# Third x group of a hybrid attention layer: its square sums, roots, normalisations and turns placed anew, and two of the cosine and sine spreads issued later

## The chip, the cores and the metric

The kernel runs on one core of a Trainium2 chip. The core's engines work side by side, each through its own instructions in order: TensorE (PE in the profile; its weight loads are PEld), VectorE (DVE), ScalarE (ACT), GpSimd (POOL) and SyncE (SP, which here only issues DMAs). They wait for each other by semaphores. The metric is the device time of one execution in microseconds (us); lower is better. Three runs of the kernel before took 1143.2 to 1147.12 us, with a median of 1145.37.

## The reference

One decoder layer over x of 2048 rows by 1024 columns, float32:

```python
mod = jax.nn.silu(c) @ w_ada[l] + b_ada[l]
shift, scale, gate = jnp.split(mod, 3, axis=-1)
h = rms_norm(x, g_pre[l]) * (1.0 + scale[:, None, :]) + shift[:, None, :]
proj = h @ w_in[l]
qa, ka, va, fa, za, qb, kb, vb, zb = jnp.split(proj, split_points, axis=-1)
oa = forgetting_attention(qa, ka, va, fa + b_fgate[l]) * silu(za)      # 8 heads of 64
qb, kb = rope(qb, positions), rope(kb, positions)
ob = sliding_window_sink_attention(qb, kb, vb, sinks[l]) * silu(zb)    # 8 query heads, 2 key heads
y = jnp.concatenate([oa, ob], axis=-1) @ w_out[l]
x = x + gate[:, None, :] * rms_norm(y, g_post[l])
```

(Reshapes are left out of these lines.) For the change, the first three matter: each row of x is divided by its root mean square, then scaled and shifted by column, and `h` is multiplied with the columns of `w_in`, of which `kb`, `vb` (with the forget gates `fa`) and `zb0` come first.

## The kernel before

**Groups and tiles.** x is handled in 16 tiles of 128 rows, x0 to x15, and these in four groups of 512 rows: group 0 is x0 to x3, group 1 x4 to x7, group 2 (the third) x8 to x11, group 3 x12 to x15. For a group the kernel does, in this order:

- `load_x` (L414): one 512 KB DMA for each tile, on SP's queue.
- `squares` (L422): the sum of squares of each row of a tile, by one ScalarE instruction with an accumulator (L429) and the reading of it; given an engine, by one VectorE instruction (L431). Both write the squares themselves into one scratch tile, `junk`, of which there is a single buffer.
- `root` (L433): on GpSimd two small instructions, mean and epsilon (L436) and the power -0.5 (L437), for the tiles of a slice of the group.
- `normal` (L439): a tile is multiplied by its root on VectorE (L445).
- `turn_x` (L470), eight times: 128 columns of all four tiles are transposed by TensorE (four matmuls with the identity, L453, into a PSUM tile `px` of five). One tick later ScalarE scales and shifts them (L461), once for odd turns, twice for even ones, and another tick later VectorE makes the low half of the float16 pair `hT` (L466, for odd turns also the high half, L465). Projections read `hT` of the group: the k-th step of a projection needs the k-th turn.

**Slices.** The early part of the kernel is a list of small TensorE pieces, `punits`; each is a slice, and `fill` (L1180) issues them in order. Ahead of a slice go the events that were set for it: `at_slice(n, f)` and the steps of the weights. After every second slice (the odd ones) a tick runs what was deferred by `after(n, f)` (L202). So the order of work on each engine's queue is written out by hand by slice numbers: an engine meets its instructions in this order, and one that waits holds up those behind it.

**The list** (L1077 to L1103), for group ci = 0, 1, 2: eight units of `kb` (L361, three matmuls each; for ci = 0 seven of them are empty), eight units of `vb` (L854, 12 matmuls each), eight units of `zb0` (L361), for ci = 2 two more such sets, of `zb0` and `zb1`; and in between the eight turns of group ci + 1, behind the units numbered in `at_`. This makes slices 0 to 31, 32 to 63 and 64 to 111. Group 1 is turned in slices 16 to 31. In slices 32 to 63 come `kb` on group 1 (32 to 39), `vb` on group 1 from slice 40, and the turns of group 2 at slices 41, 44, 47, 50, 53, 56, 59 and 62; `kb` on group 2 begins at slice 64. Group 3 is turned from slice 81 on, and `kb` on group 3 begins at slice 112.

**Events in question**, by slice: squares of x8, x9, x10, x11 at 11, 14, 33, 34, all on ScalarE; root of group 2, for all four, at 35; its normalisations at 37, 38, 39, 40; squares of x12 to x15 at 48, 50, 52, 54 on ScalarE; root of group 3 at 57; its normalisations at 66, 68, 70, 72.

**Cosines and sines.** `spread` (L475) copies a group's 32 rows of cosine and sine to all 128 partitions: eight DMAs of 64 KB from SP's queue, at slices 12, 22 and 30 for groups 1, 2 and 3. The rotation of `kb` (`evac_rope`, L797) uses them: after the last unit ScalarE copies the sums out (`qf`, L807), SP swaps halves by four DMAs (`qs`, L809), VectorE multiplies by the cosine (L812), which frees the PSUM bank, and some ticks later by the sine (L822), adds (L823), and ends in `kst` by four more DMAs (L837). For group ci the cosine is wanted a few slices behind the last `kb` unit, at slices 39, 71 and 119. The three banks `bk` of PSUM go round: a unit set takes one, and the instruction that empties it frees it.

**The maximum of a weight block.** `add` (L1021) sets the steps of each weight block by slice. For `zb1` they are written out (L1040): load at 6, `w_max` at 38 (VectorE, L236, 1.21 us, then a small DMA out on GpSimd's queue, L239), `w_back` at 46 (a DMA back to all partitions, L244, which waits for the first), `w_scale` at 67 (VectorE, L255 and four small ones), and the splitting in float16 pairs at 71 to 77. `zb1` is used first after slice 96.

Of the kernel before, what the change touches and what calls it, by code (L numbers as in the profile page):

```python
# [43 lines left out]
def hybrid_layer(  # L44
# [17 lines left out]
    V, A, G, PE, SP = nc.vector, nc.scalar, nc.gpsimd, nc.tensor, nc.sync  # L62
# [20 lines left out]
    def sm(n, tag):  # L83
        return small.tile([P, n], F32, tag=tag, name=tag)
# [131 lines left out]
    def w_load(key, pieces, eng=None):  # L216
        raw = wpool.tile([P, KT, P], F32, tag="wraw", name=f"wr_{key}")
        o = 0
        for col0, n in pieces:
            (eng or G).dma_start(raw[:, :, o:o + n], w_in0[:, col0:col0 + n].rearrange("(k p) n -> p k n", p=P))  # L220
            o += n
        wq[key] = [raw]
# [11 lines left out]
    def w_max(key):  # L234
        mx = sm(1, "w_mx")
        V.tensor_reduce(mx[:], wq[key][0][:], axis=AX.XY, op=ALU.max, apply_absolute_value=True)  # L236
        md = mx_d[len(kaps_seen) % 3]
        kaps_seen.append(key)
        G.dma_start(md[:], mx[:])  # L239
        wq[key].append(md)  # L240

    def w_back(key):
        mxr = mxp.tile([P, P], F32, tag="mxr", name="mxr")
        G.dma_start(mxr[:], wq[key].pop().rearrange("p o -> (p o)").partition_broadcast(P))  # L244
        wq[key].append(mxr)

    def w_scale(key):

        floor = key[:2] == "qk"
        raw, mxr = wq[key]  # L250
        if key in first:
            mx2 = mxr
        else:
            mx2 = sm(1, "w_mx2")
            V.tensor_reduce(mx2[:], mxr[:], axis=AX.X, op=ALU.max)  # L255
        pw = sm(1, "w_pw")
        pow2_floor(pw[:], mx2[:], "w_p2")
        if floor:
            V.tensor_tensor(pw[:], pw[:], pfl[:], op=ALU.max)
        sw = sm(1, "w_sw")  # L260
        V.reciprocal(sw[:], pw[:])
        V.tensor_scalar(sw[:], sw[:], 2.0 ** 14, None, op0=ALU.mult)
        wq[key] = [raw, pw, sw]

    def w_high(key):
        raw, pw, sw = wq[key]
        width = VB if key == "vb" else P
        pool = vbw if key == "vb" else wpq if key[0] in "qk" else wpool
        if key[:2] == "va":
            j = int(key[2:])  # L270
            if j % 2 == 0:
                wv[j // 2] = fx["wv"].tile([P, 2, KT, 2 * P], F16, tag="whl", name=f"wh_va{j}")
            whl = wv[j // 2][:, :, :, (j % 2) * P:(j % 2 + 1) * P]
        elif key == "fa":
            whl = wq["vb"][:, :, :, P:]
        else:
            whl = pool.tile([P, 2, KT, width], F16, tag="whl", name=f"wh_{key}")
        A.activation(whl[:, 0, :, 0:raw.shape[-1]], raw[:], AF.Identity, scale=sw[:])
        wq[key].append(whl)
# [65 lines left out]
    def pieces(key):  # L345
        kind, j = key[:2], int(key[2:] or 0)
        if kind == "qk":
            return [(OFF_QA + j * 64, 64), (OFF_KA + j * 64, 64)]
        return [({"qb": OFF_QB, "va": OFF_VA, "za": OFF_ZA, "zb": OFF_ZB}[kind] + j * P, P)]
# [72 lines left out]
    def squares(ci, us=range(4), eng=None):  # L422
        if ci not in rstd:
            rstd[ci] = sm(4, "ss"), sm(4, "rst")
        for u in us:
            junk = hst.tile([P, D], BF16, tag="junk", name="junk", bufs=1)
            x_, sum_ = xt[ci * 4 + u], rstd[ci][0][:, u:u + 1]
            if eng is None:
                A.activation(junk[:], x_, AF.Square, accum_out=sum_)  # L429
            else:  # L430
                eng.scalar_tensor_tensor(junk[:], x_, 1.0, x_, op0=ALU.mult, op1=ALU.mult, accum_out=sum_)  # L431

    def root(ci, us=slice(0, 4)):  # L433
        ss, rst = (t[:, us] for t in rstd[ci])
        rv = sm(4, "rs_v")[:, us]
        G.tensor_scalar(rv, ss, 1.0 / D, EPS, op0=ALU.mult, op1=ALU.add)  # L436
        G.tensor_tensor(rst, rv, mhalf[:].broadcast_to([P, us.stop - us.start]), op=ALU.pow)  # L437

    def normal(ci, us=range(4), eng=None):  # L439
        for u in us:  # L440
            t, r = ci * 4 + u, rstd[ci][1][:, u:u + 1]
            if eng is A:
                A.activation(xt[t], xt[t], AF.Copy, scale=r)
            else:
                V.tensor_scalar(xt[t], xt[t], r, None, op0=ALU.mult)  # L445
# [24 lines left out]
    def turn_x(ci, k):  # L470
        scaled, split, _ = turn(ci, k)
        after(1, scaled)
        after(2, split)

    def spread(g):  # L475

        gr, gc = slice(32 * g, 32 * g + 32), slice(g * CH, (g + 1) * CH)
        for r in range(4):
            rr = slice(32 * r, 32 * r + 32)
            SP.dma_start(cosT[rr, gc], cs_[gr, :])  # L480
            SP.dma_start(sinT[rr, gc], (sp_ if r % 2 else sn_)[gr, :])
# [537 lines left out]
    pkeys, punits = [], []  # L1019

    def add(key, us):  # L1021
        if key in ("va01", "va23"):
            for j in key[2:]:
                add(f"va{j}", [])
        elif key not in pkeys and key not in ("kb", "vb"):
            at = len(punits) - {"za3": 4}.get(key, 20 if key[:2] == "za" else 0)
            for n, (lead, f) in enumerate(((42, lambda: w_load(key, pieces(key))), (31, lambda: w_max(key)),
                                           (21, lambda: w_back(key)), (12, lambda: w_scale(key)),
                                           (9, lambda: w_high(key)), (7, lambda: w_low(key, 0)),
                                           (5, lambda: w_low(key, 1)), (4, lambda: w_done(key)))):  # L1030
                if n >= 4 and key[:2] in ("qk", "za"):
                    lead -= 1
                if n < 4 and key == "qb0":
                    lead += (16, 14, 12, 4)[n]
                if key[:2] in ("zb", "va"):
                    lead += {"va0": 26, "va2": 26, "zb3": 18}.get(key, 8)
                if n == 0 and key in ("qk1", "za0"):
                    lead += 8
                if key == "zb1":
                    lead = at - (6, 38, 46, 67, 71, 73, 75, 77)[n]  # L1040
                if key == "zb0":
                    if n >= 3:
                        events.setdefault((11, 11, 13, 14, 15)[n - 3], []).append(f)
                else:
                    events.setdefault(max(at - lead, n), []).append(f)
        if key not in pkeys:
            pkeys.append(key)
        punits.extend(us)
# [10 lines left out]
    def at_slice(n, f):  # L1059
        events.setdefault(n, []).append(f)  # L1060
# [16 lines left out]
    for ci in range(NCH):  # L1077
        n0 = len(punits)
        if ci:
            add("kb", kb_units(ci))  # L1080
        else:
            add("kb", [lambda: None] * (KT - 1) + [ku[KT - 1]])
        add("vb", vb_units(ci))
        if ci < 3:
            add(*others[ci])
            if ci == 2:
                add(*others[4])
                add(*others[5])

            mine, punits[n0:] = punits[n0:], []  # L1090
            at_ = ([15, 17, 18, 19, 20, 21, 22, 23], [8, 10, 12, 14, 16, 18, 20, 22], [16, 18, 20, 22, 24, 26, 28, 30])[ci]
            for n, u in enumerate(mine):
                punits.append(u)
                if n in at_:
                    punits.append(lambda ci=ci, k=at_.index(n): turn_x(ci + 1, k))
            if ci < 2:

                for u in range(4):
                    if ci or u:
                        at_slice(n0 + 16 + 2 * u if ci else (11, 14, 33, 34)[u], lambda ci=ci, u=u: squares(ci + 2, (u,)))  # L1100
                    at_slice(len(punits) + 2 + 2 * u if ci else len(punits) + 5 + u, lambda ci=ci, u=u: normal(ci + 2, (u,)))
                at_slice(len(punits) - 7 if ci else len(punits) + 3, lambda ci=ci: root(ci + 2))
            at_slice((12, 22, 30)[ci], lambda ci=ci: spread(ci + 1))  # L1103
    n0 = len(punits)
    at_slice(n0, lambda: open_fox())
    at_slice(n0 + 8, gates)
# [590 lines left out]
    with tc.manual_schedule():  # L1697
# [35 lines left out]
        for s, stp_ in enumerate(steps):  # L1733
            hd, r = divmod(s, NS)
            w_acc += stp_.w
            lead = 14 + min(9, max(0, s - 100) * 3 // 8)
# [114 lines left out]
```

## Time and profile before

| what | value |
|---|---|
| median of 3 runs | 1145.37 us (1143.2 to 1147.12) |
| the profiled execution | 1145.31 us |
| its span on the core | 1143.6 us, with 25130 instructions |
| mean granted TensorE clock | 0.994 |
| TensorE busy | 1116.7 us (98%) |
| VectorE busy | 902.5 us (79%) |
| ScalarE busy | 661.4 us (58%) |
| GpSimd busy | 220.6 us (19%) |
| slices 32 to 63 on TensorE | 62.78 to 88.89 us from the span's start |

How to read it: times are microseconds from the start of the span. The span is the profiled core's time from the first to the last instruction; the execution's own time is 1.7 us longer. Ends of matmuls are modelled, since they are pipelined, so their starts are compared here. `L361` is a line of the kernel. `out<-in` names the tile written and those read. The granted clock is TensorE's, as a share of full speed. The chain that ended last is followed back from the last instruction, at each step to what released it or to the instruction before it on its engine.

### The profile page before, as it was taken

What the parts mean: (1) busy time and instruction counts of PE and PEld (TensorE: products, weight loads), DVE (VectorE), ACT (ScalarE), POOL (GpSimd) and SP (SyncE); (2) the same over time, 40 slices, a digit from 0 to 9 for tenths busy, and PEclk for the clock granted to TensorE, in tenths of its full rate; (3) what the DMA queues carried; (4) which work ended last, traced back from release to release, by engine and by line L of the source; (5) the groups of instructions that cost most, each with busy time, mean ns of one, the idle gap of its engine ahead of it and who ended that gap; (6) DMA issues with size and microseconds to landing.
All of it is one profiled execution on the core that took longest, in us unless ns stands there. A gap on an engine that the chain in (4) does not pass through costs nothing.

```text
span 1143.6 us, 25130 instructions
## 1 busy us (share of the span) xinstructions
PE 1116.7 (98%) x9854; PEld 656.6 (57%) x9854; DVE 902.5 (79%) x1982; ACT 661.4 (58%) x1151; POOL 220.6 (19%) x339
## 2 busy tenths in 40 slices
PE   7889999999999999999999999999999999999997
PEld 3666545667755856555555555555556565544444
DVE  8967468968878558889888899888888998666663
ACT  3966245655555412676767666666666888633332
POOL 3111135555556420010010111001000000100000
PEclk9989999999999999999999999999999999999999
DMA  9854254423232232443244332123311237687743
GB/s 364 269 154 86 75 102 88 93 60 94 69 76 84 58 93 51 82 103 46 63 64 89 84 67 71 38 49 52 69 41 48 77 98 213 146 235 196 203 132 111
DMA packets 124365, 119.83 MB, mean 105 GB/s; under 512 B 65977, under 2 KB 101858, under 8 KB 124246
## 3 DMA queue, kind: packets, MB, share of 16 engines
q1 hardware_dynamic: 113374, 85.73, 27.5%
q0 software_dynamic: 10720, 32.46, 13.6%
q8 instruction: 77, 1.26, 0.5%
q14 instruction: 42, 0.34, 0.1%
q10 hardware_dynamic: 152, 0.04, 0.0%
HBM read 64.49 MB, written 25.18 MB: 78 GB/s over the span
## 4 chain that ended last, share of the span: by engine, by line
PE 77%; DVE 13%; DMA 4%; ACT 3%; issue 2%; SPq 1%; POOL 0%; DVEq 0%; POOLq 0%; ACTq 0%
PE bk L361 30%; PE bk L1637 13%; PE bk L379 7%; PE sta L1410 4%; PE sta L1409 4%; PE bk L1360 4%; PE poa L1435 3%; PE poa L1436 2%; PE poa L1433 2%; DVE a_m L1363 2%; PE pss L948 2%; PE bk L854 2%; PE pob L1005 1%; DVE pha L1423 1%; DMA wr_kv<-in_w_in_dram 1%
## 5 line engine op out<-in xcount | busy, mean ns | idle before, releaser
L1416 ACT ACTIVATE p<-sta,lift,scl_qk 128x1024 f32<-128x1024 f32 (+2 forms) x160 | 171.8, 1074 | 126.1 <-PE sta L1410 78.7
L361 PE MATMUL bk<-hT,wh_qk 128*128 128x512 f16 x768 | 195.4, 379 | 0.0
L1423 DVE TENSOR_TENSOR pha<-p,pha 128x1024 f16<-128x1024 f32 (+2 forms) x160 | 168.9, 1056 | 0.6 <-ACT pha L1420 0.6
L1363 DVE TENSOR_REDUCE a_m<-bk 128x1 f32<-128x512 f32 x192 | 130.3, 685 | 45.8 <-PE bk L1360 44.9
L1637 PE MATMUL bk<-wohl,oz 128*128 128x512 f16 x744 | 163.6, 379 | 1.0 <-DVE oz L1587 0.7
L1420 ACT ACTIVATE pha<-p 128x1024 f16<-128x1024 f32 (+2 forms) x160 | 148.0, 925 | 6.4 <-PE poa L1436 1.8
L1637 PEld LDWEIGHTS <-oz 128*128 128x128 f16 x744 | 70.5, 98 | 84.7 <-DVE oz L1587 1.8
L1433 PE MATMUL poa<-vt,pha 128*128 128x65 f16 x1088 | 116.6, 193 | 1.6 <-DVE ona L1442 1.6
L1436 PE MATMUL poa<-vt,pha 128*128 128x65 f16 x1088 | 116.1, 193 | 0.6 <-DVE pha L1423 0.6
L1435 PE MATMUL poa<-vt,pha 128*128 128x64 f16 x1088 | 116.6, 195 | 0.0
L361 PEld LDWEIGHTS <-wh_qk 128*128 128x128 f16 x768 | 71.7, 97 | 73.8 <-issue 2.1
L1360 PE MATMUL bk<-T 66*128 66x512 f16 (+2 forms) x320 | 110.5, 349 | 1.9 <-DVE a_m L1363 1.7
L1409 PE MATMUL sta<-T 128*128 128x512 f16 (+1 forms) x320 | 111.0, 347 | 1.1 <-ACT p L1416 0.9
L1433 PEld LDWEIGHTS <-pha 128*128 128x128 f16 x1088 | 101.5, 96 | 16.1 <-DVE ona L1442 2.4
L1410 PE MATMUL sta<-T 69*128 69x512 f16 (+1 forms) x320 | 109.9, 348 | 0.0
L1435 PEld LDWEIGHTS <-pha 128*128 128x128 f16 x1088 | 100.9, 97 | 11.6
L1436 PEld LDWEIGHTS <-pha 128*128 128x128 f16 x1088 | 100.9, 99 | 0.9 <-DVE pha L1423 0.7
L361 PE MATMUL bk<-hT,wh_za 128*128 128x512 f16 x384 | 99.8, 379 | 0.0
L379 PE MATMUL bk<-wh_va,hT 128*128 128x256 f16 x768 | 91.9, 273 | 0.0
L361 PE MATMUL bk<-hT,wh_zb 128*128 128x512 f16 x384 | 91.8, 380 | 0.0
L361 PE MATMUL bk<-hT,wh_qb 128*128 128x512 f16 x384 | 91.2, 380 | 0.0
L379 PEld LDWEIGHTS <-hT 128*128 128x128 f16 x768 | 73.3, 98 | 12.2 <-issue 2.1
(460 smaller groups left out, 1904.0 us busy)
## 6 DMA issues: line engine op xcount, KB each, us to landing
hT<-in_x_dram SPq DMA_DIRECT2D x20, 512.0 KB
wa<-in_w_ada_dram SPq DMA_DIRECT2D x16, 512.0 KB
z_d<-tz POOLq DMA_DIRECT2D x32, 256.0 KB, 3.0
T<-z_d SPq DMA_DIRECT2D x16, 512.0 KB
T<-stq SPq DMA_DIRECT2D x60, 128.0 KB
out_dram<-hT SPq DMA_DIRECT2D x15, 512.0 KB
xt<-in_x_dram SPq DMA_DIRECT2D x12, 512.0 KB
qs<-qf SPq DMA_DIRECT2D x80, 64.0 KB
```

Of the source, the lines that this page charges most:

```text
L361: PE.matmul(ps, whl[:, a, k, :], hT[ci][:, b, k, :], start=(k == 0 and n == 0), stop=(k == KT - 1 and n == 2))
L379: PE.matmul(ps[:, (u % 2) * 2 * P:(u % 2 + 1) * 2 * P], hT[ci][:, a, k, u * P:(u + 1) * P], wv[p][:, b, k, :], start=(k == 0 and n == 0), ...
L1360: PE.matmul(mx[:, :w], T[0:XM, 0, i * P:(i + 1) * P], T[0:XM, 2, pc * CH:pc * CH + w], start=True, stop=True)
L1363: V.tensor_reduce(m3[:, u, pc:pc + 1], mx[:, :w], axis=AX.X, op=ALU.max)
L1409: PE.matmul(self.st[:, o:o + w], T[:, 3, kb_], T[:, 1, qc], start=True, stop=False)
L1410: PE.matmul(self.st[:, o:o + w], T[0:XR, 2, kb_], T[0:XR, 0, qc], start=False, stop=not diag)
L1416: A.activation(self.p32[:, :self.w], self.st[:, :self.w], AF.Exp, scale=scl[f"qk{self.hd}"][:], bias=lift[:])
L1423: V.tensor_tensor(self.ph[:, 1, :self.w], self.p32[:, :self.w], self.ph[:, 0, :self.w], op=ALU.subtract)
L1433: PE.matmul(po[:, u, :], ph[:, 0, pq], vt[:, b, hd, 0:65], start=(self.first and n == 0 and u == 0), stop=False)
L1435: PE.matmul(po[:, u, 0:64], ph[:, 0, pq], vt[:, b, hd, 65:VW], start=False, stop=False)
L1436: PE.matmul(po[:, u, :], ph[:, 1, pq], vt[:, b, hd, 0:65], start=False, stop=(self.last and n == len(self.blocks) - 1))
L1637: PE.matmul(py, self.hl[:, i, k, :], w_slot(8 * j + k)[:, cc], start=(k == 0 and m_ == 0), stop=(k == KT - 1 and m_ == 2))
```

## The change

It concerns only slice numbers, the engine of some square sums, and the root of group 2, which comes in two halves:

- The squares of x11 (slice 36 instead of 34), x12 (44 instead of 48) and x13 (46 instead of 50) are taken on VectorE. Those of x14 go from slice 52 to 50; x10 (33), x15 (54), x8 (11) and x9 (14) stay on ScalarE where they were.
- Group 2 has two roots: for x8 and x9 at slice 16, for x10 and x11 at slice 37. Its normalisations come at slices 37, 37, 38 and 38.
- The turns of group 2 stand behind units 12, 14, 16, 17, 18, 19, 20 and 22: slices 45, 48, 51, 53, 55, 57, 59 and 62.
- The maximum of `zb1` is taken at slice 42, read back at 48.
- `spread` for groups 2 and 3 comes at slices 46 and 78; for group 1 it stays at 12.

The amount of work is the same, but for one root instruction pair more.

```diff
                 if key == "zb1":
-                    lead = at - (6, 38, 46, 67, 71, 73, 75, 77)[n]
+                    lead = at - (6, 42, 48, 67, 71, 73, 75, 77)[n]
...
-            at_ = ([15, 17, 18, 19, 20, 21, 22, 23], [8, 10, 12, 14, 16, 18, 20, 22], [16, 18, 20, 22, 24, 26, 28, 30])[ci]
+            at_ = ([15, 17, 18, 19, 20, 21, 22, 23], [12, 14, 16, 17, 18, 19, 20, 22], [16, 18, 20, 22, 24, 26, 28, 30])[ci]
...
                 for u in range(4):
                     if ci or u:
-                        at_slice(n0 + 16 + 2 * u if ci else (11, 14, 33, 34)[u], lambda ci=ci, u=u: squares(ci + 2, (u,)))
-                    at_slice(len(punits) + 2 + 2 * u if ci else len(punits) + 5 + u, lambda ci=ci, u=u: normal(ci + 2, (u,)))
-                at_slice(len(punits) - 7 if ci else len(punits) + 3, lambda ci=ci: root(ci + 2))
-            at_slice((12, 22, 30)[ci], lambda ci=ci: spread(ci + 1))
+                        at_slice((44, 46, n0 + 18, n0 + 22)[u] if ci else (11, 14, 33, 36)[u],
+                                 lambda ci=ci, u=u: squares(ci + 2, (u,), V if u in ((0, 1) if ci else (3,)) else None))
+                    at_slice(len(punits) + 2 + 2 * u if ci else (37, 37, 38, 38)[u], lambda ci=ci, u=u: normal(ci + 2, (u,)))
+                if ci:
+                    at_slice(len(punits) - 7, lambda: root(3))
+                else:
+                    at_slice(16, lambda: root(2, slice(0, 2)))
+                    at_slice(37, lambda: root(2, slice(2, 4)))
+            at_slice((12, 46, 78)[ci], lambda ci=ci: spread(ci + 1))
```

## The prediction

> **What bounds the kernel now.** I read the page first, its chain that ended last above all, then TensorE's waits, then the stretch in which they lie: the busy time by stretch, and the timeline of each engine. The shares of the chain by engine:
>
> ```profile
> PE 77%; DVE 13%; DMA 4%; ACT 3%; issue 2%; SPq 1%; POOL 0%; DVEq 0%; POOLq 0%; ACTq 0%
> ```
>
> TensorE carries the chain, so a change is worth the TensorE time that it saves. The change touches slices 6 to 78, and of TensorE's waits only one group lies there after 47 us: the transposes of the third x group (group 2). Four stretches around it; the columns are TensorE, its weight loads, VectorE, ScalarE and GpSimd busy with their instruction counts, granted clock, DMA share and GB/s:
>
> ```profile
> 68.00:74.00 6.00, 2.99 (x24) 2.11 (x23) 4.54 (x6) 1.13 (x2) 1.53 (x2) 0.79 0.63 145
> 74.00:80.00 6.00, 6.00 (x62) 5.92 (x61) 2.35 (x6) 2.54 (x6) 0.54 (x1) 0.64 0.36 78
> 80.00:86.00 6.00, 6.00 (x56) 4.40 (x54) 3.80 (x9) 5.97 (x13) 0.00 (x0) 1.00 0.21 12
> 86.00:92.00 6.00, 6.00 (x34) 3.23 (x32) 4.09 (x8) 5.43 (x9) 1.23 (x2) 1.00 0.38 87
> ```
>
> TensorE works 2.99 of 6 us in the first, and its granted clock is 0.79 there and 0.64 in the next. Now its timeline (start, time from first start to last end, instruction, count; in brackets the idle time before it and what ended that):
>
> ```profile
> 67.97 0.87 PE L854 MATMUL bk<-wh_vb,hT 128*128 128x136 f16 x12
> 69.84 0.30 PE L453 MATMUL px<-ident,xt 128*128 128x128 f32 x1 [1.01 <-DVE xt L445]
> 70.42 0.33 PE L453 MATMUL px<-ident,xt 128*128 128x128 f32 x1 [0.27 <-DVE xt L445]
> 72.20 0.48 PE L453 MATMUL px<-ident,xt 128*128 128x128 f32 x1 [1.46 <-DVE xt L445]
> 72.95 0.47 PE L453 MATMUL px<-ident,xt 128*128 128x128 f32 x1 [0.27 <-DVE xt L445]
> 73.22 2.93 PE L854 MATMUL bk<-wh_vb,hT 128*128 128x136 f16 x24
> 75.94 1.06 PE L453 MATMUL px<-ident,xt 128*128 128x128 f32 x4
> 76.79 2.32 PE L854 MATMUL bk<-wh_vb,hT 128*128 128x136 f16 x24
> 78.95 0.60 PE L453 MATMUL px<-ident,xt 128*128 128x128 f32 x4
> 79.39 1.58 PE L854 MATMUL bk<-wh_vb,hT 128*128 128x136 f16 x24
> 80.81 0.60 PE L453 MATMUL px<-ident,xt 128*128 128x128 f32 x4
> 81.25 0.87 PE L854 MATMUL bk<-wh_vb,hT 128*128 128x136 f16 x12
> 81.96 0.81 PE L361 MATMUL bk<-hT,wh_zb 128*128 128x512 f16 x3
> 82.61 0.60 PE L453 MATMUL px<-ident,xt 128*128 128x128 f32 x4
> ```
>
> From start to start the undisturbed paces are: a turn (four transposes) 81.25 - 80.81 = 0.44, a `vb` unit 81.96 - 81.25 = 0.71, a `zb0` unit 82.61 - 81.96 = 0.65 us. The loss against them:
>
> - After the `vb` unit the first turn should take 67.97 + 0.71 = 68.68 to 69.12. The next unit begins at 73.22: **4.10 us** lost. 3.01 of it is waiting (1.01 + 0.27 + 1.46 + 0.27), for the normalised x tiles.
> - Two `vb` units and a turn should take 1.86 us (81.25 - 79.39). They take 3.57 (73.22 to 76.79) and 2.60 (76.79 to 79.39): 1.71 + 0.74 = **2.45 us** lost to the lowered clock, with no wait left.
>
> Together **6.55 us**. Why the x tiles are late stands on the other engines. ScalarE (L429 squares x, L807 takes out `kb`), VectorE and GpSimd:
>
> ```profile
> 65.12 1.10 ACT L429 ACTIVATE junk<-xt 128x1024 bf16<-128x1024 f32 x1
> 66.07 0.25 ACT L429 ACTIVATION_READ_ACCUMULATOR junk<-xt 128x1 f32 x1
> 66.35 1.06 ACT L429 ACTIVATE junk<-xt 128x1024 bf16<-128x1024 f32 x1
> 67.31 0.19 ACT L429 ACTIVATION_READ_ACCUMULATOR junk<-xt 128x1 f32 x1
> 68.17 0.60 ACT L807 ACTIVATE qf<-bk 128x512 f32<-128x512 f32 x1 [0.66 <-PE bk L361]
> ```
>
> ```profile
> 65.78 0.69 DVE L466 TENSOR_TENSOR hT<-hf,hT 128x512 f16<-128x512 f32 x1
> 68.95 1.41 DVE L445 TENSOR_SCALAR xt<-xt,rst 128x1024 f32<-128x1024 f32 x2 [2.48 <-POOL rst L437]
> 70.28 1.21 DVE L236 TENSOR_REDUCE w_mx<-wr_zb 128x1 f32<-128x1024 f32 x1
> 71.41 1.49 DVE L445 TENSOR_SCALAR xt<-xt,rst 128x1024 f32<-128x1024 f32 x2
> ```
>
> ```profile
> 51.31 0.72 POOL L437 TENSOR_TENSOR rst<-rs_v,mhalf 128x2 f32<-128x2 f32 x1
> ...
> 67.60 0.19 POOL L436 TENSOR_SCALAR rs_v<-ss 128x4 f32<-128x4 f32 x1 [1.31 <-ACT junk L429]
> 67.87 1.04 POOL L437 TENSOR_TENSOR rst<-rs_v,mhalf 128x4 f32<-128x4 f32 x1
> 71.78 0.62 POOL L239 DMA_DIRECT2D mx_d<-w_mx  x1 [2.87 <-DVE w_mx L236]
> 79.00 0.54 POOL L244 DMA_DIRECT2D mxr<-mx_d  x1 [6.60 <-DMA mx_d<-w_mx]
> ```
>
> x10 and x11 are squared one after the other until 67.50; one root for all four tiles then ends at 68.91; VectorE, idle for 2.48 us, normalises x8 and x9, takes the maximum of `zb1` for 1.21 us, and only then x10 and x11, until 72.90.
>
> **The change part by part.**
>
> *Group 2's x.* x8 and x9 get a root of their own at slice 16, where GpSimd has nothing else: the pair at 51.31 took 0.72. x11 goes to VectorE. A squaring there stands once in the trace:
>
> ```profile
> 36.79 1.22 DVE L431 SCALAR_TENSOR_TENSOR junk<-hT 128x1024 bf16<-128x1024 f32 x1
> ```
>
> VectorE is free at 65.78 + 0.69 = 66.47, and the scratch tile `junk`, of which there is one, is free of x10's squaring at 66.32. So x11 takes 66.5 to 67.8 with the accumulator's reading, inside the old idle time. x8 and x9 follow without waiting, at some 0.72 each (two take 1.41 and 1.49 us), until 69.25. Meanwhile the pair's root: start 67.9, 0.27 to its second step (67.60 to 67.87), 0.72 for that: 68.9. x10 and x11 follow until 70.7. The maximum of `zb1` now comes behind them.
>
> *The turns.* The first turn stands behind five `vb` units instead of one: 67.97 + 5 x 0.71 = 71.52. The x tiles are there 0.8 us before. The 24 slices from the first `vb` unit on hold the same work as before, 8 x 0.71 + 8 x 0.44 + 8 x 0.65 = 14.4 us, so the next user of group 2, `kb`, begins at 82.35. Before, it began at 88.89:
>
> ```profile
> 88.89 5.34 PE L361 MATMUL bk<-hT,wh_kb 128*128 128x512 f16 x24
> ```
>
> That is 6.54 us, the same sum from the other end.
>
> *What is late next.* The turns are compressed: the first is four slices later, the last still at slice 62. Each leaves work for ScalarE and VectorE, and `kb` reads turn 7's result in its last unit, at 82.35 + 7 x 5.18/8 = 86.9. VectorE: the four stretches above hold 4.54 + 2.35 + 3.80 + 4.09 = 14.8 us of its work, nearly all of it up to turn 7's end. Three squarings are added (x11, and x12 and x13 at slices 44 and 46), 3 x 1.3 = 3.9. From 66.5 on that is 85.2 if it never waits, and about 86.1 with the waits that I see: mainly for turns 4, 6 and 7 out of ScalarE. Slack 0.8 to 1.7 us. ScalarE: 15.1 us in the same stretches, less two of its four squarings (about 1.25 each with the read), the `qf` copy and the last tanh (0.6 + 0.7), leaves 11.3; from the first turn's end at 72.15 that is 83.4, plus about 0.6 for `junk` (x14 waits until VectorE has done with x13 at 75.7) and smaller gaps: 84 to 85, in time for VectorE. I take no stall; the bounds are 0 and about 2 us.
>
> *The maximum of `zb1`.* It moves to slice 42, its reading back to slice 48, the scaling stays at slice 67. On VectorE it stands at about 71.4 to 72.6 (behind the normalised tiles and `kb`'s cosine product), its write follows on GpSimd. The times from issue to landing, over the 23 such writes and then the 23 reads of the program (min/median/max):
>
> ```profile
> DMA to landing us min/median/max: 3.5/6.7/8.9
> DMA to landing us min/median/max: 3.5/4.7/7.4
> ```
>
> From 72.6 the median is 72.6 + 6.7 + 4.7 = 84.0, the worst 88.9. VectorE comes to the scaling at 86.1 plus a tanh product (0.7) and a normalisation (0.7) = 87.5. So nothing, or 1.4 us at worst, and behind that VectorE first owes TensorE the bank that `kb` holds, which slice 80 wants at about 93.2 and VectorE, working through, would free near 91.4. Worth 0. The third group's root waits behind the reading on GpSimd; that too ends before slice 66 needs it.
>
> *Cosines and sines.* Nothing on TensorE waited for them, and groups 2 and 3 want theirs from slice 73 and 121 on. Taking 16 issues of some 0.6 us out of SP's queue lets `kb`'s swap copies leave at 68.8, when `qf` is there. The second group's issues follow at once, the third's behind the next swap copies, beside the load of `qb0`. I take 0: at most that load is late by some 2 us, before a stretch in which TensorE waited for nothing.
>
> *The price of a remaining wait.* The row at 72.20 is the first slow transpose (0.48 against 0.30), and the pace is back by 78.95: about 6.7 us at the lower clock. [...]
>
> **The rivals.**
>
> 1. *No stall* (the forecast): 1145.31 - 6.55 = **1138.8 us**. The profiled execution took 1145.31, span 1143.6, the median of the three runs is 1145.37, so the number stands for both.
> 2. *VectorE becomes the bound.* It is then busy nearly without a gap from 66.5 to 87, with 0.8 us to spare at both ends. If it slips by 1.5 to 3 us, TensorE waits 0.7 to 2.2 us in `kb`, or again at the first turn, and up to the 2.45 us of lowered clock may return: 1139.5 to 1143.4. For it: the load. Against: every duration stands in the trace.
> 3. *Given back.* TensorE arrives earlier at a thing that does not move, such as `qb0`'s weights, and waits there: about 1145. Against it: the following work on TensorE (`kb`, `vb`, turns of group 3) shows no wait in the trace, and the loads are issued by slice, so they move along.
> 4. *x12 is not there* (the slower side). ScalarE read it at 80.9; VectorE now wants it at 72.5, and behind it stand the splits of group 2. The chain shows SP released by these loads at 58.73 + 7.47 = 66.2:
>
> ```profile
> 58.73 7.47 DMA xt<-in_x_dram
> ```
>
> So it should have landed. Had it landed only by 80.9, VectorE would lose 8.4 us, 7.6 of them reaching TensorE, and with the clock's 2.45 the kernel would take 1145.31 - 6.55 + 7.6 + 2.45 = 1148.8. It turns into a loss from a landing at about 77.4 on (0.8 of slack + 6.55 - 2.45 behind 72.5).
>
> **How the numbers follow.** Forecast 0.62 (with 0.05 for a little more than it), VectorE as bound 0.22, given back 0.12, slower 0.04. About 0.3%, 3.4 us, is what a measurement of this kernel can tell from no change, so faster means below 1141.9: the forecast and most of rival 2, 0.80; within 0.16; slower 0.04. The range takes the forecast with the runs' own scatter (1143.2 to 1147.12 before) and rival 2's middle: 1136.9 to 1142.6.
>
> **What would show it.** Right: no idle time ahead of L453 around 71.5, a granted clock of 1.00 from 68 to 86, `kb`'s units on group 2 from about 82.4, and everything behind it earlier by 6.5 us. Wrong: idle time ahead of L453 on L445, ahead of L361 on L466, a clock below 1.00 there (rival 2); L431 waiting for a DMA (rival 4); or a new wait between 90 and 150 us (rival 3).

## The result and the profile after

The changed kernel takes 1138.74 us (median of six runs, 1137.31 to 1141.07), the kernel before, with it, 1145.05 (six runs, 1143.2 to 1147.12). The ratio is 0.9947, with a 95% interval of 0.9931 to 0.9963: 6.3 us faster, where 6.55 was forecast. The profiled execution happens to be the slowest of the six, 1141.07 us with a span of 1139.3, so its span isn't set against the span before; the stretch of the change is.

TensorE in that stretch, the rows that answer to those before (start, time from first start to last end, instruction, count):

```profile
68.07 3.71 PE L854 MATMUL bk<-wh_vb,hT 128*128 128x136 f16 x60
71.62 0.60 PE L453 MATMUL px<-ident,xt 128*128 128x128 f32 x4
72.06 1.58 PE L854 MATMUL bk<-wh_vb,hT 128*128 128x136 f16 x24
73.48 0.60 PE L453 MATMUL px<-ident,xt 128*128 128x128 f32 x4
...
82.43 5.34 PE L361 MATMUL bk<-hT,wh_kb 128*128 128x512 f16 x24
87.61 5.84 PE L854 MATMUL bk<-wh_vb,hT 128*128 128x136 f16 x96
```

There are no brackets: the four transposes of the first turn follow one another, and nothing on TensorE waits. Busy time by stretch of the same execution (TensorE, weight loads, VectorE, ScalarE, GpSimd, then clock, DMA share, GB/s):

```profile
68.00:74.00 6.00, 6.00 (x96) 5.90 (x94) 5.39 (x9) 2.49 (x5) 2.18 (x3) 1.00 0.25 59
74.00:80.00 6.00, 6.00 (x48) 4.40 (x47) 5.93 (x15) 5.43 (x10) 0.00 (x0) 1.00 0.35 77
80.00:86.00 6.00, 6.00 (x32) 3.05 (x31) 5.34 (x10) 5.03 (x9) 1.96 (x3) 1.00 0.44 93
```

The clock, 0.79 and 0.64 before, is 1.00. VectorE, at 4.54, 2.35 and 3.80 us before, is now nearly full.

The cleanest measure is one inside an execution, since starts shift by over a us from one to the next: from the first `vb` unit on group 1 to the first on group 2. After, 87.61 - 68.07 = 19.54 us. Before:

```profile
94.07 5.84 PE L854 MATMUL bk<-wh_vb,hT 128*128 128x136 f16 x96
```

94.07 - 67.97 = 26.10 us. The difference is 6.56. In what follows this time is called the stage; 19.54 is a stage without a wait. It is read from one execution of each kernel; the runs' medians tell whether the others agree. VectorE and GpSimd in it:

```profile
66.51 1.22 DVE L431 SCALAR_TENSOR_TENSOR junk<-xt 128x1024 bf16<-128x1024 f32 x1
67.66 0.08 DVE L431 DVE_READ_ACCUMULATOR junk<-xt 128x1 f32 x1
67.66 1.41 DVE L445 TENSOR_SCALAR xt<-xt,rst 128x1024 f32<-128x1024 f32 x2
69.68 1.42 DVE L445 TENSOR_SCALAR xt<-xt,rst 128x1024 f32<-128x1024 f32 x2 [0.61 <-POOL rst L437]
71.01 0.68 DVE L812 SCALAR_TENSOR_TENSOR qc<-bk,cosT 128x512 f32<-128x512 f32 x1
71.61 1.21 DVE L236 TENSOR_REDUCE w_mx<-wr_zb 128x1 f32<-128x1024 f32 x1
...
76.16 0.69 DVE L822 TENSOR_TENSOR qs<-qs,sinT 128x512 f32<-128x512 f32 x1
...
84.95 0.69 DVE L466 TENSOR_TENSOR hT<-hf,hT 128x512 f16<-128x512 f32 x1
```

```profile
67.84 0.62 POOL L436 TENSOR_SCALAR rs_v<-ss 128x2 f32<-128x2 f32 x1 [1.42 <-DVE junk L431]
68.54 1.10 POOL L437 TENSOR_TENSOR rst<-rs_v,mhalf 128x2 f32<-128x2 f32 x1
73.11 0.62 POOL L239 DMA_DIRECT2D mx_d<-w_mx  x1 [3.47 <-DVE w_mx L236]
80.83 0.55 POOL L244 DMA_DIRECT2D mxr<-mx_d  x1 [7.10 <-DVE hT L465]
```

x11's squaring goes where VectorE was idle (2.48 us before); x10 and x11 are normalised at 71.1 (forecast 70.7), half a us ahead of the turn; the split of turn 7 ends at 85.6 (forecast 86.1), where the last unit of `kb` wants it at 82.43 + 4.53 = 87.0. One thing is new: the root's two instructions take 0.62 and 1.10 us, not 0.19 and 0.72, and VectorE waits 0.61 us for them.

### The profile page after: what moved, and what is told of

Read it like the earlier page. It is cut to its first block, busy times and chain, and to the rows that moved or that the text cites. A ratio compares the mean times of both kernels' runs of the same rounds, so it can differ in the third digit from the quotient of the medians.

```text
span 1139.3 us, 25131 instructions
## 1 busy us (share of the span) xinstructions
PE 1113.6 (98%) x9854; PEld 654.2 (57%) x9854; DVE 905.8 (80%) x1988; ACT 659.1 (58%) x1145; POOL 222.7 (20%) x341
## 4 chain that ended last, share of the span: by engine, by line
PE 79%; DVE 12%; DMA 3%; ACT 3%; issue 2%; POOL 1%; DVEq 0%; POOLq 0%; ACTq 0%
PE bk L361 30%; PE bk L1642 13%; PE bk L379 7%; PE sta L1415 5%; PE sta L1414 5%; PE bk L1365 4%; PE poa L1440 3%; PE poa L1441 3%; PE poa L1438 3%; DVE a_m L1368 2%; PE bk L854 2%; PE pss L948 2%; PE pob L1005 1%; DVE pha L1428 1%; PE px L453 1%
```

## The experiments

The theory was that TensorE lost its time to late tiles and to the lowered clock that followed, and that of the change the turns and the order on VectorE matter while the spreads are worth nothing. The stage lengths and ratios of all of them:

| run | what | stage, us | ratio to before (95%) |
|---|---|---|---|
| e0 | the changed kernel again | 19.54 | 0.9946 (0.9933 to 0.9958) |
| e1 | before, turns moved | 26.70 | 1.0004 (0.9995 to 1.0012) |
| e2 | changed, turns back | 21.63 | 0.9972 (0.9962 to 0.9982) |
| e3 | changed, both spreads back | 24.01 | 0.9999 (0.9989 to 1.001) |
| e4 | changed, group 2's squares, root, normalisations back | 19.84 | 0.9954 (0.9942 to 0.9966) |
| e5 | changed, group 3's squares back on ScalarE | 19.54 | 0.9949 (0.9937 to 0.9962) |
| e6 | changed, x8 and x9 normalised earlier | 19.54 | 0.9951 (0.9938 to 0.9963) |
| e7 | changed, all of group 3 squared on VectorE | 19.54 | 0.9945 (0.9932 to 0.9959) |
| e8 | before, spreads moved | 24.93 | 1.0001 (0.9991 to 1.001) |
| e9 | before, turns and spreads moved | 20.64 | 0.9959 (0.9946 to 0.9973) |
| e11 | changed, group 2's spread back | 19.54 | 0.996 (0.9947 to 0.9974) |
| e12 | changed, group 3's spread back | 19.54 | 0.9952 (0.994 to 0.9965) |

Each ratio is to the kernel before on the same chip; a stage is that of the one profiled execution.

**e1, only the turns moved.**

```diff
-  [8, 10, 12, 14, 16, 18, 20, 22]
+  [12, 14, 16, 17, 18, 19, 20, 22]
```

> The kernel before with the eight turns of group 2 at their new slices and nothing else. [...] The clock stays at 1.00. About 1141.5 us, half to two thirds of the gain. Rival 1 (the clock drops on any wait above 1 us): another 2 us or more, 1143.5 to 1144.5. Rival 2 (later turns are all that matters): 1138.7.

Nothing is gained: the median is 1144.98 us, where about 1141.5 was expected. The profiled execution took 1147.87, above that, so its waits may be longer than in most. The wait at the first turn has shrunk to 0.7 us, but TensorE waits in `kb` instead. Its timeline there, and then VectorE's:

```profile
84.36 0.81 PE L361 MATMUL bk<-hT,wh_kb 128*128 128x512 f16 x3
87.86 0.38 PE L361 MATMUL bk<-hT,wh_kb 128*128 128x512 f16 x1 [2.69 <-DVE hT L465]
88.59 0.81 PE L361 MATMUL bk<-hT,wh_kb 128*128 128x512 f16 x3 [0.35 <-DVE hT L466]
89.73 5.96 PE L361 MATMUL bk<-hT,wh_kb 128*128 128x512 f16 x17 [0.33 <-DVE hT L466]
```

```profile
75.68 0.69 DVE L466 TENSOR_TENSOR hT<-hf,hT 128x512 f16<-128x512 f32 x1 [0.77 <-ACT hf L461]
86.06 0.69 DVE L822 TENSOR_TENSOR qs<-qs,sinT 128x512 f32<-128x512 f32 x1 [9.69 <-DMA qs<-qf]
```

VectorE stands 9.69 us at the sine product of `kb` on group 1, for the swap copies `qs`, and behind it stand the splits of turns 1 to 7. The sign of this wait was expected, its size was not: 1 to 2 us of TensorE's time was put down for it, and it is 3.4. The `kb` units after the wait are slow too (17 matmuls from 89.73 in 5.96 us, where 24 take 5.34): the clock, expected to stay at 1.00, is 0.81 from 86 to 92 and 0.91 from 92 to 98 (rows further down). The gain went into a new wait, and the clock fell again.

**e3, both spreads back in the changed kernel.**

```diff
-  at_slice((12, 46, 78)[ci], lambda ci=ci: spread(ci + 1))
+  at_slice((12, 22, 30)[ci], lambda ci=ci: spread(ci + 1))
```

> The changed kernel with the cosine and sine spreads at their old slices 22 and 30. The prediction's step (the spreads are worth nothing): 1138.7 us. Rival: with VectorE nearly full, the swap copies of kb, which then leave SP only at 74.8 to 77.2 instead of 68.9 to 71.4, hold VectorE at the sine product from 76.2 to about 79; what is behind it comes some 2.5 us later, turn 7's split ends at about 88 instead of 85.6, and TensorE, which wants it at 87.0, waits about 1 us in kb: 1139.7 to 1140.

The whole gain is gone, by the ratio. SP's issues around the swap copies (L809), and VectorE's wait:

```profile
67.65 2.69 SPq L837 DMA_DIRECT2D kst<-stb  x4
70.38 0.61 SPq L480 DMA_DIRECT2D cosT<-cs__365  x1
...
75.98 0.59 SPq L481 DMA_DIRECT2D sinT<-sp__363  x1
76.67 2.44 SPq L809 DMA_DIRECT2D qs<-qf  x4
```

```profile
83.31 0.69 DVE L822 TENSOR_TENSOR qs<-qs,sinT 128x512 f32<-128x512 f32 x1 [6.39 <-DMA qs<-qf]
```

`qf` was there at 69.6 (ScalarE's copy, 68.97 for 0.60), the swap copies are issued from 76.67 on because eight spread issues stand ahead of them, and land 4.2 us after the last of them has been issued. TensorE then waits seven times in `kb`, 3.1 us in all, and the stage is 24.01. The rival was right in its place and too small in its price: VectorE was to wait from 76.2 to about 79 and TensorE about 1 us; 6.39 and 3.1 us came. What the stage still saves in this execution, 2.1 us, the runs' times don't show. Its span, 1142.9 us, is only 0.7 below that of before, in part because `kb` on group 1 began at 63.59, 0.8 us later than before. The wait also differs behind the same order on SP (9.69 in e1, 6.39 here): the four issues of the swap copies took 5.69 us in e1 and 2.44 here. Why, and how long the other executions wait, no trace shows.

**e8, only the spreads moved.**

```diff
-  at_slice((12, 22, 30)[ci], lambda ci=ci: spread(ci + 1))
+  at_slice((12, 46, 78)[ci], lambda ci=ci: spread(ci + 1))
```

> The kernel before with only the two cosine and sine spreads moved. Theory (they matter only where kb's sine product is early on VectorE; in the kernel before it stands at 81.7, after the late turns): TensorE's waits on L445 and the lowered clock stay as they were, ratio to before 0.9985 to 1.0015. Rival (the traffic of the spreads itself made group 2's tiles late): the wait on L445 shrinks and the time falls by 2 us or more, ratio 0.998 or less.

No gain: the transposes wait 3.1 us on L445, as before. So the spreads did not make the tiles late; alone they free something that nobody wants yet, since in the kernel before the late turns put off the sine product to 81.7. The stage is 24.93, not 26.10, with the same wait: less time was lost to the clock (rows further down). The time shows nothing of this.

**e9, turns and spreads moved, the rest as before** (both edits above on the kernel before).

> The kernel before with the turns of group 2 and the two spreads moved; squares, root, normalisations and zb1's maximum as before. Theory (turns and spreads together carry the gain): the last tile of group 2 is normalised about 4.2 us after the last slice of kb on group 1 has ended, where the turn comes after 3.6, so TensorE waits 0.7 us in all as it did with the turns alone, and the wait for the swap copies is gone; ratio to before 0.9950 to 0.9962, some 5 us of gain. Rival (the rest of the change is needed): four squares on ScalarE make turn 7 late by 2 us or more, ratio 0.997 or above.

As the theory had it: 0.9959, about three quarters of the gain, with 0.7 us of waiting left at the first turn:

```profile
72.05 0.33 PE L453 MATMUL px<-ident,xt 128*128 128x128 f32 x1 [0.32 <-DVE xt L445]
72.71 0.33 PE L453 MATMUL px<-ident,xt 128*128 128x128 f32 x1 [0.33 <-DVE xt L445]
```

The stage is 20.64, that is 1.1 us longer than in the changed kernel; the intervals of the ratios overlap. Four squarings on ScalarE don't hold the turns up.

**e2, the turns back.**

```diff
-  [12, 14, 16, 17, 18, 19, 20, 22]
+  [8, 10, 12, 14, 16, 18, 20, 22]
```

> The changed kernel with the turns of group 2 at their old slices. Theory: the tiles are ready at about 71.1 as in the changed kernel, the first turn comes at 68.7, so TensorE waits about 2.1 us; a gap this short leaves the clock at 1.00, so 1138.7 + 2.1 = 1140.8 us. Rival (a wait of 2 us already lowers the clock): about 2.4 us more, 1143.2.

The stage of the profiled execution is 21.63, 2.09 us longer, as expected to the tenth. The clock is 1.00 all through:

```profile
66.55 0.87 PE L854 MATMUL bk<-wh_vb,hT 128*128 128x136 f16 x12
67.26 0.67 PE L453 MATMUL px<-ident,xt 128*128 128x128 f32 x2
68.95 0.33 PE L453 MATMUL px<-ident,xt 128*128 128x128 f32 x1 [1.03 <-DVE xt L445]
69.62 0.33 PE L453 MATMUL px<-ident,xt 128*128 128x128 f32 x1 [0.33 <-DVE xt L445]
69.78 1.58 PE L854 MATMUL bk<-wh_vb,hT 128*128 128x136 f16 x24
```

So of the 6.56 us, 2.09 come from the later turns, and with the turns at their old places the order on VectorE (and the spreads, which must not be late) still saves the other 4.5, the clock's share included. By the runs' times, 0.9972 is 3.2 us of gain, 1.3 less than the stage's. The profiled execution took 1140.02 us; the median is 1141.89, where 1140.8 was expected, and where the other executions lost that no trace shows.

**e4, group 2's squares, root and normalisations back.**

```diff
-  at_slice((44, 46, n0 + 18, n0 + 22)[u] if ci else (11, 14, 33, 36)[u],
-           lambda ci=ci, u=u: squares(ci + 2, (u,), V if u in ((0, 1) if ci else (3,)) else None))
-  at_slice(len(punits) + 2 + 2 * u if ci else (37, 37, 38, 38)[u], lambda ci=ci, u=u: normal(ci + 2, (u,)))
+  at_slice((44, 46, n0 + 18, n0 + 22)[u] if ci else (11, 14, 33, 34)[u],
+           lambda ci=ci, u=u: squares(ci + 2, (u,), V if u in ((0, 1) if ci else ()) else None))
+  at_slice(len(punits) + 2 + 2 * u if ci else (37, 38, 39, 40)[u], lambda ci=ci, u=u: normal(ci + 2, (u,)))
...
-  at_slice(16, lambda: root(2, slice(0, 2)))
-  at_slice(37, lambda: root(2, slice(2, 4)))
+  at_slice(35, lambda: root(2))
```

> The changed kernel with group 2's squares (all on ScalarE), single root (slice 35) and normalisations (slices 37 to 40) as before; turns, zb1's maximum, spreads and group 3's squares as changed. Theory: the root ends at 68.9, and with the maximum out of the way the four normalisations run from there to 71.8; the first turn comes at 71.6, so TensorE waits 0.2 us or nothing: 1138.7 to 1139.0 us. Rival (halved root and VectorE's squaring carry the gain): a wait of 1 us or more at the first turn, 1139.8 us or above.

0.9954, a stage of 19.84: 0.3 us longer, all of it in the first turn, whose gaps are too short to be listed (0.74 us to the next unit instead of 0.44). The halved root and the squaring of x11 on VectorE are worth those 0.3 us, as long as the maximum of `zb1` no longer stands between the normalisations. Against e9 (20.64), which has it between them, and group 3's squares on ScalarE too, 0.8 us are left for that maximum, since e5 shows that the other difference costs nothing; it was not moved by itself.

**e5, group 3's squares back on ScalarE, and e7, all of them on VectorE.**

```diff
-  at_slice((44, 46, n0 + 18, n0 + 22)[u] if ci else (11, 14, 33, 36)[u],
-           lambda ci=ci, u=u: squares(ci + 2, (u,), V if u in ((0, 1) if ci else (3,)) else None))
+  at_slice((48, 50, 52, 54)[u] if ci else (11, 14, 33, 36)[u],
+           lambda ci=ci, u=u: squares(ci + 2, (u,), V if u in (() if ci else (3,)) else None))
```

> The changed kernel with all of group 3's squares on ScalarE at slices 48 to 54 as before. Theory (one engine's load replaces the other's): ScalarE has 2.4 us more between the first and the last turn, its last scaling ends at about 86 instead of 84.5, VectorE has 2.6 us less; turn 7's split ends at about 87 where TensorE wants it at 87.0: a wait of 0 to 0.5 us, ratio to before 0.9945 to 0.9955. Rival (VectorE's squarings of x12 and x13 are what makes room): a wait of 1.5 us or more in kb, ratio 0.996 or above.

And e7:

```diff
-           lambda ci=ci, u=u: squares(ci + 2, (u,), V if u in ((0, 1) if ci else (3,)) else None))
+           lambda ci=ci, u=u: squares(ci + 2, (u,), V if u in ((0, 1, 2, 3) if ci else (3,)) else None))
```

> The changed kernel with x14 and x15 squared on VectorE too, so that all of group 3 is. Theory (VectorE is then the bound of the turns): in the changed kernel turn 7's split ends 3.2 us after kb on group 2 begins, and is wanted after 4.5; two squarings are 2.6 us more, of which 0.5 goes into VectorE's two short waits for ScalarE, so it ends at about 5.2 and TensorE waits 0.7 us in all: ratio to before about 0.9955. Rival (ScalarE, which has 2.4 us less, brings the turns forward by as much): no wait, ratio 0.9947.

Both have a stage of 19.54 and the changed kernel's time. The last split of turn 7, of e5 and then of e7:

```profile
84.39 0.69 DVE L466 TENSOR_TENSOR hT<-hf,hT 128x512 f16<-128x512 f32 x1
```

```profile
84.91 0.69 DVE L466 TENSOR_TENSOR hT<-hf,hT 128x512 f16<-128x512 f32 x1
```

`kb` on group 2 begins at 80.92 and 80.98. So the split ends 4.2 us after it in e5, 4.6 in e7, against 3.2 in the changed kernel, and it is wanted some 4.5 us after it. Moving x12 and x13 gives about 1 us of slack that nothing used; two squarings more take it all, and no wait shows yet. e7's 0.7 us of waiting did not come: the split was forecast at 5.2.

**e11 and e12, one spread back.**

```diff
-  at_slice((12, 46, 78)[ci], lambda ci=ci: spread(ci + 1))
+  at_slice((12, 22, 78)[ci], lambda ci=ci: spread(ci + 1))
```

> The changed kernel with only group 2's spread back at slice 22, group 3's at 78. Theory (what costs 5 us is the place in SP's queue: 16 issues between the loads of x and kb's swap copies are 10 us of issuing, 8 are 5): SP issues the eight from 59 to 67, kb's stores behind them, and the swap copies leave at about 70 to 72.5; VectorE waits at the sine product 0 to 1 us, TensorE nothing: ratio to before 0.9945 to 0.9955. Rival (this one spread, whose copies meet the x loads on the DMA engines, is what costs): VectorE waits 3 us or more, ratio 0.998 or above.

And e12:

```diff
-  at_slice((12, 46, 78)[ci], lambda ci=ci: spread(ci + 1))
+  at_slice((12, 46, 30)[ci], lambda ci=ci: spread(ci + 1))
```

> The changed kernel with only group 3's spread back at slice 30, group 2's at 46. Theory (as above): SP issues the eight in the idle time that it has, from about 63.6 to 68.7, and the swap copies leave at 69 to 71.5 as in the changed kernel: ratio to before 0.9945 to 0.9955. Rival (this one, just ahead of the swap copies, is what costs): VectorE waits 3 us or more at the sine product, ratio 0.998 or above.

Neither makes VectorE wait, both have a stage of 19.54. Before the swap copies SP has room for eight issues, but not for 16: in e11 group 2's end ahead of `kb`'s stores, in e12 group 3's fill SP's idle time, whose last row and the swap copies are:

```profile
67.80 0.59 SPq L481 DMA_DIRECT2D sinT<-sp__363  x1
68.49 3.52 SPq L809 DMA_DIRECT2D qs<-qf  x4
```

In both the swap copies are issued from about 68.5 on. Counted from the first `vb` unit of the same execution that is 2.0 us in e11 and 1.8 in e12, against 7.9 in e3 and 0.8 in the changed kernel. So in these executions neither spread by itself was the cost, but both together ahead of one transfer that has to be early. For e11 that stays in part open: its ratio lies just above the 0.9945 to 0.9955 that were expected, and its median, 1140.41 us of 1137.52 to 1140.6, is some 2.5 us above those of e0, e7 and e12. The profiled execution took 1137.52, so it can't show where the others lost time; the intervals overlap.

**e6, x8 and x9 normalised at slice 35.**

```diff
-  (37, 37, 38, 38)[u]
+  (35, 35, 38, 38)[u]
```

> The changed kernel with the normalisations of x8 and x9 at slice 35, ahead of x11's squaring, so that VectorE runs nothing while GpSimd takes the second root of group 2. In the changed kernel that root took 0.62 and 1.10 us beside VectorE's normalisations, against 0.19 and 0.72 us elsewhere. Theory (VectorE's normalisations hold GpSimd up): the two instructions take 0.19 and 0.7 us here. Rival (what slows them is something else, such as the DMA issued before them): 0.6 and 1.1 us again. The time: the last tile is ready at about 71.7, the turn comes at 71.6, so the same as the changed kernel within 0.3 us, ratio to before about 0.995.

VectorE is idle for 1.12 us while GpSimd takes the root, and the root's instructions are short again:

```profile
67.53 0.19 POOL L436 TENSOR_SCALAR rs_v<-ss 128x2 f32<-128x2 f32 x1 [2.75 <-DVE junk L431]
67.81 0.71 POOL L437 TENSOR_TENSOR rst<-rs_v,mhalf 128x2 f32<-128x2 f32 x1
```

So each of the two instructions took 0.4 us longer beside VectorE's normalisations (0.62 and 1.10 in the changed kernel). The time is the changed kernel's.

**e0, the changed kernel beside e7, e11 and e12.**

> The changed kernel as it is, beside the other three: ratio to before about 0.9947, no wait of TensorE between 60 and 150 us, and VectorE not waiting for the swap copies.

It repeats: 0.9946, and 1137.78 us against 1143.69. Its profile has the stage of 19.54 too. Two waits of 0.6 us of L948 on ScalarE, which the first profile of the changed kernel shows between 150 and 212 us and the one before doesn't, aren't in it: they belong to that execution, not to the change.

## Why the prediction was right, and where it was not

**The loss and its end.** Right. The loss was read as 4.10 us at the first turn (3.01 of it waiting) and 2.45 of lowered clock behind it: 6.55. The stage shortened by 6.56, counted from the same execution of before, so this agreement tests only that nothing waits after the change; the runs' medians, 6.3 us, are the other test. `kb` on group 2 began 14.36 us after the first `vb` unit, where 14.4 was worked out.

**Group 2's tiles.** Right in order, 0.4 us off in time: the step "0.27 to its second step (67.60 to 67.87), 0.72 for that: 68.9" took a root beside idle engines for one beside VectorE's normalisations, and it ended at 69.64. The slack before the first turn was 0.5 us, not 0.8.

**What is late next.** Right: no stall. The slack behind turn 7 was 1.3 us, within 0.8 to 1.7.

**The maximum of `zb1`.** Right: it was taken from 71.6 to 72.8, read back from 80.8, and L255 found it at 86.8 without a wait. e9 and e4 add what the prediction had not priced: that it left its place between the normalisations is worth about 0.8 us.

**Cosines and sines: this step failed.** "Nothing on TensorE waited for them ... I take 0." Alone it is 0 (e8), but the change without it gains nothing (e3, e1). The prediction saw that the swap copies would leave at 68.8, and did not ask what would happen if they did not: the sine product, which the trace of before shows at 81.7 with its data there, comes at 76.2 as soon as the turns are on time, and the swap copies of the old order land at 83 to 86. It was a cover that the change itself takes away. That the total came out right is luck in this step: the change moves the spreads too, and by the prediction's working it would have been given the same 6.55 us without them.

**The clock.** The term was right in size for that execution; what a wait costs in clock no run shows as a rule. In before no single wait is longer than 1.46 us, and the clock is at half from 71.50 to 78.32, 6.8 us, where about 6.7 was read from the pace (columns as above; TensorE's busy time is the first after the comma, the clock the last number but two):

```profile
71.50:74.91 3.41, 2.43 (x17) 2.08 (x18) 1.99 (x3) 1.44 (x2) 0.62 (x1) 0.50 0.49 108
74.91:78.32 3.41, 3.41 (x29) 3.35 (x28) 1.13 (x3) 0.78 (x2) 0.00 (x0) 0.50 0.45 97
```

The stretches of 6 us around the waits of e8, e1, e2 and e3:

```profile
68.00:74.00 6.00, 3.54 (x25) 2.94 (x26) 4.55 (x7) 1.45 (x2) 1.15 (x1) 0.76 0.43 100
74.00:80.00 6.00, 6.00 (x82) 5.66 (x80) 3.29 (x9) 4.17 (x8) 0.55 (x1) 0.96 0.16 36
```

```profile
86.00:92.00 6.00, 3.31 (x9) 0.99 (x9) 5.84 (x13) 4.49 (x8) 1.49 (x2) 0.81 0.05 13
92.00:98.00 6.00, 5.89 (x55) 3.78 (x54) 5.61 (x14) 3.14 (x5) 1.54 (x2) 0.91 0.45 120
```

```profile
68.00:74.00 6.00, 4.71 (x67) 4.49 (x68) 5.64 (x8) 2.90 (x6) 0.73 (x2) 1.00 0.37 86
```

```profile
80.00:86.00 6.00, 4.47 (x25) 2.40 (x23) 2.62 (x6) 1.24 (x3) 0.54 (x1) 1.00 0.15 14
86.00:92.00 6.00, 4.66 (x18) 1.64 (x17) 5.71 (x12) 5.69 (x10) 1.49 (x2) 1.00 0.37 87
```

Where TensorE worked 2.99 of 6 us (before), 3.54 (e8) and 3.31 (e1), the clock was 0.79, 0.76 and 0.81, and 0.64, 0.96 and 0.91 in the 6 us behind; where it worked 4.71 (e2, with a wait of 1.03 us), 4.47 and 4.66 (e3), it was 1.00. So the sum of the waits does not give the price: about 3 us at the same place went with 0.79 and 0.64 in before and with 0.76 and 0.96 in e8 (stages of 26.10 and 24.93), and 3.1 us spread over 8 us with 1.00 in e3. What decides it the runs don't show. The 2.45 us of the prediction belong to that execution.

**The rivals.** VectorE as the bound did not come about, though e7 uses its slack up. "Given back" did not come: the time saved in the stage is saved in the runs, 6.56 us beside 6.3. x12 was there: L431 took it at 72.73 with no wait for a DMA.

## What to carry to other kernels

When a stall is taken away, look at each instruction that will then be early, on every engine's queue, and ask when its data comes now: a transfer that was hidden by the stall becomes the next one. What an edit is worth depends on its partner: here the turns alone and the spreads alone gave nothing, and both together most of the gain, so an edit priced at nothing needs the price of its absence too. Where issues of about 0.6 us each stand ahead of an urgent one on a queue, count them: here eight fitted (e11 and e12), 16 were too many (e3).

## What the runs showed of the hardware

- Two small GpSimd instructions took 0.62 and 1.10 us beside two float32 normalisations on VectorE (the changed kernel), and 0.19 and 0.71 us beside an idle VectorE (e6): 0.4 us less for each.
- Four swap copies of 64 KB landed 4.2 us after the last had been issued in e3 (issue ends at 79.1, VectorE goes on at 83.3).
- TensorE's granted clock in two successive stretches of 6 us was 0.79 and 0.64 in before (68 to 80, 3.0 us of waiting), 0.76 and 0.96 in e8 (68 to 80, 3.1 us from 67.4 on), 0.81 and 0.91 in e1 (86 to 98, where the longest wait, 2.69 us, ended at 87.86), and 1.00 in both in e3 (80 to 92), whose 3.1 us of waiting were spread over 8 us.
